# One weight group in three: the low part added up by a DMA instead of subtracted on VectorE

## The chip, the cores and the metric

The kernel runs on one core of a Trainium2 chip. The time is device microseconds of one execution, taken as the median of several runs; lower is better. TensorE (PE) multiplies, VectorE (DVE) and ScalarE (ACT) work elementwise, GpSimd (POOL) does a few small operations, and SyncE (SP) issues the loads. Sixteen DMA engines carry the transfers of all queues.

## The reference: one decoder layer on 256 tokens

The layer has a width of 2048. One projection of `x` makes the inputs of two token mixers, an mLSTM with 4 heads and a retention with 8 heads; their outputs are projected, gated, merged, projected again and normalised with the residual. A feed-forward part of width 8192 with a squared ReLU and a second norm follow:

```
u  = x @ w_in + b_in                      # 2048 -> 16392 columns
ya = head_norm(mlstm(...)) * sigmoid(mo) @ w_branch_m
yb = head_norm(retention(...)) * silu(rg) @ w_branch_r
y  = (sigmoid(ga) * ya + sigmoid(gb) * yb) @ w_out + b_out
h  = layer_norm(alpha * x + y)
out = layer_norm(alpha * h + relu(h @ w1 + b1)**2 @ w2 + b2)
```

All of it is float32. The weights of these products are some 319 MB, each read once.

## The kernel before

The float32 products are made of three passes of a shorter float format (`F32R`): each operand is split in a high part, which is the value rounded to that format, and a low part, value minus high part, and a product is high by high, low by high and high by low.

**The stream of weights.** The weights lie in memory as 608 groups of 128 x 1024 float32 (512 KB), in the order of use. `load_until` has SP load group `g` into one of four buffers `raw` (L94 to L96). `split_until` makes the two parts: ACT casts `raw` to `whi` (L111), and then DVE subtracts, `wlo = raw - whi` (L112). `whi` and `wlo` have three buffers each (`ring`, L65), so a group's parts can be made when TensorE has done with the parts of the group three places before. `next_w` (L131) asks for the split of group `g + 2` when group `g` is handed to TensorE, so parts are at most two groups ahead. A few groups at the two norms go to wider places instead of the ring (`hold`, tile name `held`).

**Two ways of use.** In `w_stationary` (L137) the weights are the stationary operand: a group is 8 pairs of matmuls, one of 512 columns with `whi` (L145) and one of 256 with `wlo` (L147), and two groups make a block of 128 output rows, followed by elementwise work on ACT and DVE (in the feed-forward part `up`: `t` L728 and L729, `sg` L732, `y` L734, `hT` L735 and L736). In `x_stationary` (L153) and `x_split` (L172) the activations are stationary and a group is 12 matmuls of 512 columns, each set of three being L164 (`whi`), L165 (`whi`), L166 (`wlo`).

**What sets the order.** Each engine works through its own list in order, and a scheduler sets where the lists' rows stand from the order of the program. Work of the heads and transposes is slipped in between groups by generators (`step`). POOL's list before holds only four constants, 16 small `pow` operations (`rstd_of`, L363) and four multiply-adds at the very end (L762, L763). SP's list holds the loads, each waiting until its buffer is free.

Of the kernel before, what the change touches and what calls it, by code (L numbers as in the profile page):

```python
# [10 lines left out]
F32 = mybir.dt.float32  # L11
F32R = mybir.dt.float32r
I32 = mybir.dt.int32
AF = mybir.ActivationFunctionType
OP = mybir.AluOpType
PSUM = bass.MemoryType.PSUM

P = 128
T = 256
D = 2048  # L20
KB = D // P
# [18 lines left out]
def layer_kernel(ctx: ExitStack, tc: tile.TileContext, xT, x, pos, wp, wg, cols, rows, b_in, b_ff1, gbias,  # L40
                 cst, decay, sel, out):
    nc = tc.nc
    V, S, TE, G = nc.vector, nc.scalar, nc.tensor, nc.gpsimd
# [10 lines left out]
    def big(name):  # L54
        return s16.tile([P, 4096], F32, tag="s16", name=name)

    def pair(name):
        return t32.tile([P, KB, 2, T], F32R, tag="t32", name=name)

# [1 line left out]
    NG = wp.shape[0]  # L61
    RAW_B, HL_B = 4, 3
    raws, parts, place = {}, {}, {}
# [1 line left out]
    def ring():  # L65
        return (wpool.tile([P, GW], F32R, tag="whi", bufs=HL_B, name="whi"),
                wpool.tile([P, GW], F32R, tag="wlo", bufs=HL_B, name="wlo"))

    def hold(first, sizes):
        for pool, n in sizes:  # L70
            box = []

            def view(i, pool=pool, n=n, box=box):
                if not box:
                    tag = {t32: "t32", s16: "s16"}[pool]
                    box.append(pool.tile([P, n, 2, GW], F32R, tag=tag, name="held"))
                return box[0][:, i, 0], box[0][:, i, 1]

            for i in range(n):
                place[first + i] = lambda i=i, view=view: view(i)  # L80
            first += n
    state = {"dma": 0, "split": 0, "use": 0}

    def pieces(g):
        n = GW // 2 if g < 3 or G_FF <= g < G_FF + 4 else GW
        return [slice(i, i + n) for i in range(0, GW, n)]

    def load_until(n):
        while state["dma"] < min(n, NG):
            g = state["dma"]  # L90
            if g < KB // 2:
                k = slice(2 * g, 2 * g + 2)
                nc.sync.dma_start(xraw[:, k], xT[:, k])
            r = wpool.tile([P, GW], F32, tag="raw", bufs=RAW_B, name="raw")  # L94
            for c in pieces(g):
                nc.sync.dma_start(r[:, c], wp[g, :, c])  # L96
            raws[g] = r
            state["dma"] += 1

    def split_until(n):  # L100
        while state["split"] < min(n, NG):
            g = state["split"]
            load_until(g + 1)
            hi, lo = place.pop(g)() if g in place else ring()
            r = raws.pop(g)
            if g < KB // 2:
                k = slice(2 * g, 2 * g + 2)
                S.copy(xs[:, k, 0], xraw[:, k])
                V.tensor_tensor(xs[:, k, 1], xraw[:, k], xs[:, k, 0].bitcast(F32), OP.subtract)
            for c in pieces(g):  # L110
                S.copy(hi[:, c], r[:, c])  # L111
                V.tensor_tensor(lo[:, c], r[:, c], hi[:, c].bitcast(F32), OP.subtract)  # L112
            parts[g] = (hi, lo)
            state["split"] += 1
            load_until(g + 1 + RAW_B)
# [15 lines left out]
    def next_w():  # L131
        g = state["use"]
        split_until(g + HL_B)
        state["use"] += 1
        return parts.pop(g)
# [62 lines left out]
        return ([(g, h) for h in range(2) for g in range(HOLD)],  # L198
                [(g, h) for g in range(HOLD, n) for h in range(2)])

# [1 line left out]
    xraw = big("xraw").rearrange("p (k t) -> p k t", k=KB)  # L202
    xs = pair("xs")
    warm = cp.tile([P, 1], F32, name="warm")
# [1 line left out]
    S.activation(warm, warm, AF.Sigmoid)  # L206
    load_until(RAW_B)
    split_until(HL_B)
    wg_t = cp.tile([P, KB, 8], F32, name="wg_t")
    nc.sync.dma_start(wg_t, wg)  # L210
# [19 lines left out]
    def rows_bc(dst, i):  # L230
        nc.sync.dma_start(dst, bass.AP(tensor=rows.tensor, offset=rows.offset + i * D, ap=[[0, P], [1, D]]))

# [1 line left out]
    ex = cp.tile([P, MH, 384], F32, name="ex")  # L234
    em = cp.tile([P, 2, MH], F32, name="em")
    cos_t = cp.tile([P, T], F32, name="cos_t")
# [119 lines left out]
        yield  # L356
        V.tensor_scalar(sin_t, sin_t, col[:, C_SIGN:C_SIGN + 1], None, OP.mult)

# [1 line left out]
    def rstd_of(dst, var, n):  # L360
        v = sm.tile([P, n], F32, tag=f"ve{n}", name="ve")
        V.tensor_scalar(v, var, EPS, None, OP.add)
        G.tensor_tensor(dst, v, nhalf[:, :n], OP.pow)  # L363
# [118 lines left out]
                V.scalar_tensor_tensor(dst[:, eb + i, 1], t, g, dst[:, eb + i, 0].bitcast(F32),  # L482
                                       OP.mult, OP.subtract)

# [1 line left out]
    def halves(t):  # L486
        return t.rearrange("p (a b) -> p a b", a=2)

# [56 lines left out]

    x_stationary(xs, KB, 4, mo_chunk)

# [1 line left out]
    hmT = []  # L549
    rqk = big("rqk").rearrange("p (k t) -> p k t", k=16)  # L550

# [25 lines left out]

    x_stationary(xs, KB, 4, rg_chunk)

# [1 line left out]
    def gate(dst, c0):  # L581
        def consume(blk, ps):
            t = wk.tile([P, T], F32, tag="t1", name="t1")
            S.activation(t, ps[:, T:], AF.Copy)
            V.tensor_tensor(t, ps[:, :T], t, OP.add)
            S.activation(dst[:, blk], t, AF.Sigmoid, bias=col[:, c0 + blk:c0 + blk + 1])
        return consume
# [4 lines left out]
    sgb = big("sgb").rearrange("p (k t) -> p k t", k=16)  # L592
    w_stationary(xs, 16, gate(sgb, C_BIN + 48))

# [1 line left out]
    hrT = []  # L596

    def branch_m(blk, ps):
# [27 lines left out]

    w_stationary(hrT[0], 16, branch_r)

# [1 line left out]
    hold(G_OUT + 24 + 8 - HOLD, [(s16, 2), (s16, 2), (s16, 2)])  # L630
    hold(G_FF, [(s16, 2), (s16, 2), (s16, 2)])
    st1 = sm.tile([P, 2, 4, 6], F32, tag="st1", name="st1", bufs=2)
# [48 lines left out]

    x_split(mgT, *late(KB), first_norm)

# [1 line left out]
    hT = pair("hT")  # L685
    brow = wk.tile([P, 512], F32, tag="brow", name="brow")
    nc.sync.dma_start(brow, bass.AP(tensor=b_ff1.tensor, offset=b_ff1.offset, ap=[[0, P], [1, 512]]))
# [18 lines left out]
    b2 = big("b2")[:, 0:D]  # L706
# [62 lines left out]
    x_split(hT, *late(KB), second_norm)  # L769


# [1 line left out]
def _stat(w):  # L773
    k, n = w.shape
    return w.reshape(k // P // 8, 8, P, n // P, P).transpose(3, 0, 2, 1, 4).reshape(-1, P, GW)


def _move(w):
    k, n = w.shape
    return w.reshape(k // P // 2, 2, P, n // 512, 512).transpose(3, 0, 2, 1, 4).reshape(-1, P, GW)  # L780


def _constants():
    s = np.arange(P)
    cst = np.zeros((P, 3, P), np.float32)
    cst[:, 0] = np.eye(P)
    cst[:, 1] = s[:, None] <= s[None, :]
    cst[:, 2] = 1.0
    lg = np.log1p(-(2.0 ** (-5.0 - np.arange(RH))))
    rel = np.arange(T)[None, :] - s[:, None]  # L790
    dec = np.where(rel >= 0, np.exp(np.maximum(rel, 0)[None] * lg[:, None, None]), 0.0) * RDQK ** -0.5
    dec = np.concatenate([dec, dec[:, :, :P]], axis=2).transpose(1, 0, 2).astype(np.float32)
    sel = np.zeros((MH, MH, P), np.float32)
    for h in range(MH):
        sel[h, h] = 1.0
    half = RDQK // 2
    invf = np.power(10000.0, -np.arange(half) / half).astype(np.float32)
    fc = np.stack([np.concatenate([invf, invf]),
                   np.concatenate([-np.ones(half), np.ones(half)]).astype(np.float32)], axis=1)
    return cst, np.ascontiguousarray(dec), sel, fc.astype(np.float32)  # L800


def _lay_out(i):
    w_in, b_in = np.asarray(i["w_in"])[0], np.asarray(i["b_in"])[0]
    w1, w2 = np.asarray(i["w_ff1"])[0], np.asarray(i["w_ff2"])[0]
    c = lambda o, n: w_in[:, o:o + n]  # noqa: E731
    parts = [_move(c(O_MV, D)), _stat(c(O_MQ, D)), _move(c(O_MO, D)), _stat(c(O_RQ, D)), _move(c(O_RV, D)),
             _move(c(O_RG, D)), _stat(c(O_GA, 2 * D)), _stat(np.asarray(i["w_branch_m"])[0]),
             _stat(np.asarray(i["w_branch_r"])[0]), _move(np.asarray(i["w_out"])[0])]
    for q in range(4):  # L810
        f = slice(q * D, (q + 1) * D)
        up = [_move(w1[:, :512]), _stat(w1[:, 512:D])] if q == 0 else [_stat(w1[:, f])]
        parts += up + [_move(w2[f])]
    wp = np.concatenate(parts, axis=0)
    x = np.asarray(i["x"])[0]
    cst, dec, sel, fc = _constants()
    b2 = lambda v: np.asarray(v).reshape(-1, P).T  # noqa: E731
    cols = np.concatenate([
        b2(b_in[O_MQ:O_MQ + D]), b2(b_in[O_RQ:O_RQ + D]), b2(b_in[O_GA:O_GA + 2 * D]),
        *[b2(np.asarray(i["m_conv_w"])[0][k]) for k in range(CONV_K)], b2(np.asarray(i["m_conv_b"])[0]),  # L820
        b2(np.asarray(i["m_norm_g"])[0]), b2(np.asarray(i["r_norm_g"])[0]), b2(np.asarray(i["b_ff1"])[0]), fc,
        b2(np.asarray(i["ln1_g"])[0]), b2(np.asarray(i["ln1_b"])[0])], axis=1)
    rows = np.stack([np.asarray(i[n])[0] for n in ("b_out", "ln1_g", "ln1_b", "b_ff2", "ln2_g", "ln2_b")])
    return {
        "xT": x.T.reshape(KB, P, T).transpose(1, 0, 2), "x": x, "pos": np.asarray(i["positions"])[0], "wp": wp,
        "wg": w_in[:, O_GI:O_GI + 8].reshape(KB, P, 8).transpose(1, 0, 2), "cols": cols, "rows": rows, "b_in": b_in, "b_ff1": np.asarray(i["b_ff1"])[0][:512],
        "gbias": b_in[O_GI:O_GI + 8], "cst": cst, "decay": dec, "sel": sel,
    }
# [15 lines left out]
```

## Time and profile before

| | before |
|---|---|
| median of 2 runs | 1762.16 us (1761.91 to 1762.40) |
| span of the profiled execution | 1760.6 us; nothing of that execution is known outside its span |
| PE busy | 1740.9 us (99%) |
| PEld busy (weight loads, beside PE) | 1475.3 us (84%) |
| DVE busy | 1111.0 us (63%) |
| ACT busy | 840.7 us (48%) |
| POOL busy | 19.7 us (1%) |
| DMA, share of 16 engines | 56.7% on the one queue of the loads |
| mean granted TensorE clock | 0.998 of 2.4 GHz |

Busy shares are means over the whole span. A row of a timeline gives the start, the duration and what the instruction makes of what. Matmul durations overlap, so the step from one start to the next is a matmul's cost.

### The profile page before, as it was taken

The numbers are of one execution on the slowest core, as the hardware profiler recorded it, in microseconds if no ns is written. First come the engines' busy times: TensorE is split into PE (matmuls) and PEld (weight loads), VectorE is DVE, ScalarE is ACT, GpSimd is POOL, SyncE is SP. The second block draws the span as 40 slices with busy tenths as digits, with TensorE's granted clock in tenths as the row PEclk, the third lists the DMA queues.
The fourth block names the chain that finished last, engine by engine and source line by source line (L and its number), as shares of the span: only waits on it lengthen the run. The fifth ranks groups of instructions, "written<-read, shape, count | busy, mean of one in ns | idle before, by whom it ended". The sixth has DMA issues, their size and how long they took to land.

```text
span 1760.6 us, 23131 instructions
## 1 busy us (share of the span) xinstructions
PE 1740.9 (99%) x8882; PEld 1475.3 (84%) x8882; DVE 1111.0 (63%) x1535; ACT 840.7 (48%) x1144; POOL 19.7 (1%) x24
## 2 busy tenths in 40 slices
PE   8999999999999999999999999999999999999997
PEld 6888888888888888888888878888888888888885
DVE  5788766875566645466666578655665566556656
ACT  5454444654444544554444465534553455345532
POOL 0000000000000000000000000000000000000001
PEclk9999999999999999999999999999999999999999
DMA  8565545456665456555555557555555555555553
GB/s 288 177 205 188 194 166 167 168 191 203 205 206 187 163 183 238 184 193 189 188 186 189 199 186 280 192 192 192 184 188 194 191 189 187 195 191 183 189 193 130
DMA packets 96439, 339.44 MB, mean 193 GB/s; under 512 B 10820, under 2 KB 12868, under 8 KB 95304
## 3 DMA queue, kind: packets, MB, share of 16 engines
q1 hardware_dynamic: 96328, 337.97, 56.7%
q8 instruction: 69, 1.13, 0.2%
q14 instruction: 42, 0.34, 0.1%
HBM read 335.83 MB, written 2.10 MB: 192 GB/s over the span
## 4 chain that ended last, share of the span: by engine, by line
PE 58%; issue 40%; DVE 1%; POOL 0%; ACT 0%; DMA 0%; SPq 0%; POOLq 0%; ACTq 0%
PE ps_w L145 20%; PE ps_w L147 10%; PE ps_x L164 8%; PE ps_x L165 8%; PE ps_x L166 8%; PE tp L475 0%; PE n L375 0%; PE ps_x L187 0%; PE ps_x L186 0%; PE ps_x L185 0%; PE n L376 0%; PE n L377 0%; PE gp L247 0%; PE sp L382 0%; DVE xr L766 0%
## 5 line engine op out<-in xcount | busy, mean ns | idle before, releaser
L112 DVE TENSOR_TENSOR wlo<-raw,whi 128x1024 fp32r<-128x1024 f32 (+1 forms) x593 | 722.7, 1219 | 545.3 <-ACT whi L111 541.8
L111 ACT CAST whi<-raw 128x1024 fp32r<-128x1024 f32 (+1 forms) x593 | 619.8, 1045 | 706.1 <-PE ps_x L165 377.2
L145 PE MATMUL ps_w<-xs,whi 128*128 128x512 f32 x1024 | 363.4, 399 | 0.0
L145 PE MATMUL ps_w<-x1T,whi 128*128 128x512 f32 x960 | 338.1, 397 | 0.0
L147 PE MATMUL ps_w<-xs,wlo 128*128 128x256 f32 x1024 | 287.6, 281 | 0.0
L147 PE MATMUL ps_w<-x1T,wlo 128*128 128x256 f32 x960 | 269.5, 281 | 0.0
L145 PEld LDWEIGHTS ps_w<-xs,whi 128*128 128x128 f32 x1024 | 192.4, 188 | 47.0
L145 PEld LDWEIGHTS ps_w<-x1T,whi 128*128 128x128 f32 x960 | 180.2, 188 | 43.9
L164 PE MATMUL ps_x<-whi,xs 128*128 128x512 f32 x512 | 201.8, 394 | 4.9 <-ACT whi L111 4.9
L165 PE MATMUL ps_x<-whi,xs 128*128 128x512 f32 x512 | 200.6, 392 | 0.0
L166 PE MATMUL ps_x<-wlo,xs 128*128 128x512 f32 x512 | 200.1, 391 | 0.0
L147 PEld LDWEIGHTS ps_w<-xs,wlo 128*128 128x128 f32 x1024 | 193.5, 189 | 0.1
L165 PE MATMUL ps_x<-whi,hT 128*128 128x512 f32 x480 | 186.8, 389 | 0.0
L164 PE MATMUL ps_x<-whi,hT 128*128 128x512 f32 x480 | 186.8, 389 | 0.0
L166 PE MATMUL ps_x<-wlo,hT 128*128 128x512 f32 x480 | 186.7, 389 | 0.0
L145 PE MATMUL ps_w<-yT,whi 128*128 128x512 f32 x512 | 181.8, 400 | 0.0
L147 PEld LDWEIGHTS ps_w<-x1T,wlo 128*128 128x128 f32 x960 | 181.4, 189 | 0.2
L147 PE MATMUL ps_w<-yT,wlo 128*128 128x256 f32 x512 | 143.8, 281 | 0.0
L164 PEld LDWEIGHTS ps_x<-whi,xs 128*128 128x128 f32 x512 | 96.8, 189 | 25.5 <-ACT whi L111 5.0
L145 PEld LDWEIGHTS ps_w<-yT,whi 128*128 128x128 f32 x512 | 96.2, 188 | 23.5
L166 PEld LDWEIGHTS ps_x<-wlo,xs 128*128 128x128 f32 x512 | 96.8, 189 | 20.6 <-DVE wlo L112 0.2
L165 PEld LDWEIGHTS ps_x<-whi,xs 128*128 128x128 f32 x512 | 96.9, 189 | 19.7
(246 smaller groups left out, 1546.5 us busy)
## 6 DMA issues: line engine op xcount, KB each, us to landing
raw<-in_wp SPq DMA_DIRECT2D x601, 512.0 KB, 3.4
brow<-in_b_in SPq DMA_DIRECT2D x16, 256.0 KB, 4.4
gb<-in_rows SPq DMA_DIRECT2D x4, 1024.0 KB, 8.2
raw<-in_wp SPq DMA_DIRECT2D x14, 256.0 KB, 4.6
xraw<-in_xT SPq DMA_DIRECT2D x8, 256.0 KB, 6.5
xr<-in_x SPq DMA_DIRECT2D x1, 2048.0 KB
dec<-in_decay SPq DMA_DIRECT2D x8, 192.0 KB, 3.1
bob<-in_rows SPq DMA_DIRECT2D x1, 1024.0 KB, 5.4
```

The source lines that it names most:

```text
L111: S.copy(hi[:, c], r[:, c])
L112: V.tensor_tensor(lo[:, c], r[:, c], hi[:, c].bitcast(F32), OP.subtract)
L145: TE.matmul(ps, hi[:, c], src[:, kb].rearrange("p a t -> p (a t)"), start=kb == 0, stop=False)
L147: TE.matmul(ps[:, :T], lo[:, c], src[:, kb, 0], start=False, stop=kb == KB - 1)
L164: TE.matmul(ps[half], src[:, kb, 0, t], hi[:, w], start=first, stop=False)
L165: TE.matmul(ps[half], src[:, kb, 1, t], hi[:, w], start=False, stop=False)
L166: TE.matmul(ps[half], src[:, kb, 0, t], lo[:, w], start=False, stop=last)
```

## The change

For each group with `g % 3 == 2`, from group 16 to group 591 and where the group is one piece, `split_until` now has ACT write the negated raw weights, rounded to the short format, into the low part's buffer, ACT cast the high part as before, and POOL issue a DMA that adds the raw weights onto the negated high part in SBUF. The subtraction on DVE is gone for these groups. This holds for 191 groups: 103 of `w_stationary`, 85 of `x_stationary` and `x_split` in the ring, and 3 held ones. Comment lines fall away elsewhere, so a line from L118 on has a number higher by 5.

```diff
-            for c in pieces(g):
-                S.copy(hi[:, c], r[:, c])
-                V.tensor_tensor(lo[:, c], r[:, c], hi[:, c].bitcast(F32), OP.subtract)
+            if g % 3 == 2 and KB <= g < NG - 16 and len(pieces(g)) == 1:
+                S.activation(lo, r, AF.Copy, scale=-1.0)
+                S.copy(hi, r)
+                G.dma_start(lo.bitcast(F32), r, accum_op=OP.add)
+            else:
+                for c in pieces(g):
+                    S.copy(hi[:, c], r[:, c])
+                    V.tensor_tensor(lo[:, c], r[:, c], hi[:, c].bitcast(F32), OP.subtract)
             parts[g] = (hi, lo)
             state["split"] += 1
             load_until(g + 1 + RAW_B)
```

The list of ACT in an `x_stationary` product of the feed-forward part, before (numbers after a name tell buffers apart):

```order
L111 CAST whi_10471<-raw_10399 128x1024
L111 CAST whi_10489<-raw_10417 128x1024
L111 CAST whi_10507<-raw_10435 128x1024
L111 CAST whi_10525<-raw_10453 128x1024
L111 CAST whi_10543<-raw_10475 128x1024
L111 CAST whi_10561<-raw_10493 128x1024
```

The same stretch of ACT's list now:

```order
L116 CAST whi_10451<-raw_10378 128x1024
L116 CAST whi_10469<-raw_10396 128x1024
L112 CAST whi_10487<-raw_10414 128x1024
L111 ACTIVATE wlo_10488<-raw_10414 128x1024
L116 CAST whi_10506<-raw_10433 128x1024
L116 CAST whi_10524<-raw_10455 128x1024
L112 CAST whi_10542<-raw_10473 128x1024
L111 ACTIVATE wlo_10543<-raw_10473 128x1024
```

One group in three has the negation (L111) right behind its cast (L112), and the groups that follow have moved down by one row.

The list of ACT in `w_stationary` of the feed-forward part (`t1` is the tile that the profile names `t`), before:

```order
L111 CAST whi_9574<-raw_9470 128x1024
L728 ACTIVATE t1_9564<-ps_w_9519 128x256
L732 ACTIVATE sg_9567<-t1_9564,col_136 128x256
L111 CAST whi_9596<-raw_9492 128x1024
L735 CAST hT_9181<-y_9569 128x256
```

The same part of the program now:

```order
L112 CAST whi_9984<-raw_9869 128x1024
L733 ACTIVATE t1_9969<-ps_w_9924 128x256
L111 ACTIVATE wlo_9985<-raw_9869 128x1024
L737 ACTIVATE sg_9972<-t1_9969,col_136 128x256
L116 CAST whi_10007<-raw_9892 128x1024
L740 CAST hT_9293<-y_9974 128x256
L116 CAST whi_10039<-raw_9929 128x1024
L733 ACTIVATE t1_10029<-ps_w_9983 128x256
L737 ACTIVATE sg_10032<-t1_10029,col_136 128x256
L111 ACTIVATE wlo_10062<-raw_9951 128x1024
L740 CAST hT_9293<-y_10034 128x256
L112 CAST whi_10061<-raw_9951 128x1024
```

Where the changed group is the first of its block, the negation stands behind `t`; where it is the second, it stands behind `sg` and ahead of `hT`, and its own cast comes two rows later. On POOL's list there is one DMA for each changed group, 191 in all, each with a wait for ACT.

## Rows read from the trace of the kernel before

**Rows 1.** The page, parts 1 and 2 (40 slices of the span).
```profile
span 1760.6 us, 23131 instructions
PE 1740.9 (99%) x8882; PEld 1475.3 (84%) x8882; DVE 1111.0 (63%) x1535; ACT 840.7 (48%) x1144; POOL 19.7 (1%) x24
...
PE   8999999999999999999999999999999999999997
...
PEclk9999999999999999999999999999999999999999
```

**Rows 2.** The page, part 4, shares of the chain that ended last.
```profile
PE 58%; issue 40%; DVE 1%; POOL 0%; ACT 0%; DMA 0%; SPq 0%; POOLq 0%; ACTq 0%
```

**Rows 3.** The page, part 5: busy us, mean ns of one, idle before.
```profile
L112 DVE TENSOR_TENSOR wlo<-raw,whi 128x1024 fp32r<-128x1024 f32 (+1 forms) x593 | 722.7, 1219 | 545.3 <-ACT whi L111 541.8
L111 ACT CAST whi<-raw 128x1024 fp32r<-128x1024 f32 (+1 forms) x593 | 619.8, 1045 | 706.1 <-PE ps_x L165 377.2
```

**Rows 4.** Timeline of an x_stationary product: start us, us, engine, line.
```profile
1317.14 0.39 PE L164 MATMUL ps_x<-whi,hT 128*128 128x512 f32 x1
...
1317.15 1.05 ACT L111 CAST whi<-raw 128x1024 fp32r<-128x1024 f32 x1 [1.67 <-PE ps_x L165]
...
1317.59 0.39 PE L166 MATMUL ps_x<-wlo,hT 128*128 128x512 f32 x1
...
1318.24 1.22 DVE L112 TENSOR_TENSOR wlo<-raw,whi 128x1024 fp32r<-128x1024 f32 x1 [1.50 <-ACT whi L111]
...
1319.86 0.39 PE L164 MATMUL ps_x<-whi,hT 128*128 128x512 f32 x1
```

**Rows 5.** Timeline of w_stationary, the `up` product of the feed-forward part.
```profile
1272.31 0.40 PE L145 MATMUL ps_w<-x1T,whi 128*128 128x512 f32 x1
...
1272.44 1.05 ACT L111 CAST whi<-raw 128x1024 fp32r<-128x1024 f32 x1 [1.23 <-issue]
...
1272.55 0.28 PE L147 MATMUL ps_w<-x1T,wlo 128*128 128x256 f32 x1
...
1273.40 0.38 ACT L728 ACTIVATE t<-ps_w 128x256 f32<-128x256 f32 x1
...
1275.12 0.51 ACT L732 ACTIVATE sg<-t,col 128x256 f32<-128x256 f32 x1 [1.35 <-DVE t L729]
...
1275.14 0.40 PE L145 MATMUL ps_w<-x1T,whi 128*128 128x512 f32 x1
```

**Rows 6.** Queues (packets, MB, share) and issues (us to landing) of DMA.
```profile
q1 hardware_dynamic: 96328, 337.97, 56.7%
...
raw<-in_wp SPq DMA_DIRECT2D x601, 512.0 KB, 3.4
...
bob<-in_rows SPq DMA_DIRECT2D x1, 1024.0 KB, 5.4
```

**Rows 7.** Tile `raw`, all its loads.
```profile
DMA to landing us min/median/max: 3.0/3.4/9.2
```

**Rows 8.** Tile `gb`, its four loads of 1024 KB.
```profile
DMA to landing us min/median/max: 4.5/8.2/10.9
```

**Rows 9.** Timeline of POOL, the shortest `pow`.
```profile
584.15 0.69 POOL L363 TENSOR_TENSOR rs<-ve,nhalf 128x2 f32<-128x2 f32 x1 [2.82 <-DVE ve L362]
```

**Rows 10.** Waits of SP's queue: us in total, times, longest.
```profile
SPq L96 <- DVE wlo L112: 857.1, 361, 7.6
```

**Rows 11.** Windows: us, busy (count) of PE, PEld, DVE, ACT, POOL, then clock, DMA.
```profile
1038.00:1040.00 2.00, 0.61 (x3) 0.19 (x2) 2.00 (x8) 2.00 (x4) 0.11 (x1) 1.00 0.00 0
...
1748.00:1750.00 2.00, 0.47 (x3) 0.05 (x1) 1.93 (x4) 0.00 (x0) 0.00 (x0) 1.00 0.70 265
1750.00:1752.00 2.00, 0.00 (x0) 0.00 (x0) 1.50 (x6) 0.00 (x0) 1.05 (x1) 0.96 0.29 112
1752.00:1754.00 2.00, 0.00 (x0) 0.00 (x0) 2.00 (x4) 0.79 (x1) 1.03 (x1) 0.50 0.00 0
```

## The prediction, made before the result was known

> **What bounds the kernel now.** I read the page's busy shares first. TensorE is busy for 1740.9 us of 1760.6, evenly over the slices, with the clock fully granted [rows 1]; all the idle time of TensorE is 20 us. The chain that ended last gives PE 58% and "issue" 40% [rows 2]; the second is the step between pipelined matmuls of the same engine, so TensorE is bound by its own matmuls. VectorE, at 63%, spends 722.7 us on the subtractions and sits idle ahead of them for 545 us until the cast on ScalarE is done; ScalarE sits idle ahead of its casts for 706 us, mostly until TensorE lets go of a buffer [rows 3]. So the split of the weights is paced by TensorE, and an engine relieved of a subtraction saves nothing. What the change can do is to make a low part late.
>
> **How much time a low part has.** Two timelines show the beat. In an x_stationary product a group begins at 1317.14 and the next at 1319.86, so a group takes 2.72 us; its first use of a low part comes 0.45 us after its start (1317.59). The cast at 1317.15 serves the group that begins two groups later, at 1322.58, and the first low matmul of that group is due at 1323.03 [rows 4]. The subtraction that starts at 1318.24 ends at 1319.46: 3.6 us to spare. In w_stationary a group takes 1275.14 - 1272.31 = 2.83 us, and the first low matmul comes 0.24 us after the start [rows 5].
>
> **The change, part by part.**
> - *Removed:* 191 subtractions of 1.22 us, 233 us of VectorE [rows 3]. Worth nothing: they end 3.6 us ahead of their use.
> - *Added on ScalarE:* 191 negations of a 128 x 1024 tile. No such row exists; the cast of the same tile takes 1.05 us [rows 4], and I take that. The 200 us bring ScalarE from 48% to 59% of the old span. Its idle time covers that, but the negation lies in the path of the low part, ahead of the DMA. A negation waits for TensorE's last use of the old low part; the casts behind it wait for a later release anyway.
> - *Added on POOL:* 191 DMAs, each waiting for the negation. The 16 `pow` operations share this queue, and some now stand behind a DMA that waits; between heads there is room for some us, at the two norms one DMA can add a negation's wait. I cost this at under 10 us.
> - *Raw buffers:* a `raw` of a changed group is freed by the landing of the accumulate and not by VectorE, and SP, which issues in order and waits now for VectorE (857 us over 361 loads, [rows 10]), waits there with the next loads behind it. Working with the landing time taken below: the accumulate that starts at 1319.25 lands 6.1 us later, at 1325.35; the load that reuses the buffer takes 3.4 [rows 6] and lands at 1328.75. Its cast is four groups after 1317.15, at 1328.03, plus the stall of 2.3 us that this landing causes, 1330.3. So it stays hidden, by 1.6 us.
>
> **The path of a changed low part.** From the negation's end to the first low matmul, the DMA has:
> - x_stationary: cast 1317.15 to 1318.20, negation to 1319.25, due at 1323.03: **3.78 us**.
> - w_stationary, first group of a block (52 groups): cast from 1272.44, then `t`, which ends at 1273.78, negation to 1274.83; due at 1272.31 + 5.66 + 0.24 = 1278.21: **3.38 us**.
> - w_stationary, second group (51): the negation stands behind `sg`, which ends at 1275.63, and ends at 1276.68; its old buffer is free from 1275.14; due at 1275.14 + 5.66 + 0.24 = 1281.04: **4.36 us**.
> - The 3 held groups don't wait for a ring buffer: no stall.
>
> If the time L from the negation's end to the landing is longer than that, TensorE waits for the rest, once in each changed group: the negation of the next changed group waits until TensorE has gone through this one, so a stall is never made up.
>
> **What L is.** No row shows an accumulating DMA or one issued by POOL. Below, L is no less than the fastest plain load of the same 512 KB, 3.0 us [rows 7]. Above, I take the slowest 1024 KB load among other loads, 10.9 us [rows 8], and a POOL operation of 0.69 us for the issue [rows 9], 11.6 in all. The nearest row is the 1024 KB load that landed in 5.4 us [rows 6], since an accumulate of 512 KB reads the raw tile and the old low part, 1024 KB. With 0.7 us for the issue on POOL, **L = 6.1 us**.
>
> The Trainium skill, page "DMA: Bandwidth & Descriptors", section "Anatomy of one DMA — SWDGE (gpsimd) path", fits a DMA issued by GpSimd as 2.0 us plus its bytes at 436 GB/s. By that my estimate for 512 KB is 3.2 us, the accumulate would be hidden in all three places and the time would be 1762 us; for 1024 KB it is 4.4 us. No run here shows such a DMA yet.
>
> **The sum.** With L = 6.1 a stall is 2.32 us in x_stationary (85 groups), 2.72 us and 1.74 us in w_stationary (52 and 51):
>
> 85 x 2.32 + 52 x 2.72 + 51 x 1.74 = 197 + 141 + 89 = 427 us.
>
> Span 1760.6 + 427 = 2188 us. The runs' median lies 1.6 us over the profiled span, so 2190 us. The `pow` waits of under 10 us are within the range.
>
> **Rivals.**
> 1. *Not slower: the accumulate lands in time.* The point of decision is L of 3.4 to 4.4 us. For it: plain loads land in 3.0 to 3.4 us, and the DMA engines are free 43% of the time [rows 6, 7]. Against it: these numbers are for half the bytes read, and from a queue that needs no work of POOL. At L of 3.4 or less no group stalls, and the time is 1762 us; VectorE's freed 233 us give nothing. At L = 4.0 the sum is 52 x 0.62 + 85 x 0.22 = 51 us, which is 1813 us. That rule of the Trainium skill (the page on DMA, same section) is this rival's mechanism. Chance 0.11, of which 0.01 lies between 2% slower and 1813 us.
> 2. *Much slower: the adding itself is slow.* 96328 packets took 56.7% of 16 engines, 166 ns each [rows 6]; a tile of 128 rows is 8 packets on each engine, 1.3 us. At twice that for an accumulate, it adds 191 x 2.66 = 507 us to 998 us of each engine, which is still under the span. If adding needs four or more times a packet, or if POOL is slow to make up the DMA, L goes to 8 and more; at the bound of 11.6 the stalls are 7.82, 8.22 and 7.24 us, 1461 us in all, so 3223 us. At such gaps TensorE's clock can fall as well: after the last matmul, in 1748 to 1750, the grant was 0.96 in the next two us and then 0.50, which is 1.2 GHz, while 1.4 us of idle time in 1038 to 1040 left it at 1.00 [rows 11]. At the lower level a group takes another 2.72 us; once in each changed group that would be 520 us more, part of which the next DMA gets back as time to land. Gaps of 2.3 us lie between those rows, and I count the clock as kept there. Chance 0.09.
> 3. *In between, by the lock of a port.* VectorE is busy 63%, with 1.22 us operations [rows 1, 3]; if POOL had to wait for the end of one each time it makes up a DMA, L is up to 7.3 and the sum up to 188 x 1.2 = 226 us more, 2415 us. I have no row for such a wait. It is part of the forecast's range. The Trainium skill, page "SBUF — State Buffer", section "🔬 SBUF: two separate sides", says that GpSimd can't write descriptors during VectorE's two-port modes; no run here shows it.
>
> That the change does nothing it says can be left out: POOL's list has the 191 DMAs, and VectorE's has 191 subtractions fewer.
>
> **How the numbers follow.** The forecast, that the accumulate lands late and TensorE waits in each of the 188 ring groups, has a chance of 0.80, with L between 4.0 and 9.6 us. These ends give 1813 us (above) and 85 x 5.82 + 52 x 6.22 + 51 x 5.24 = 1085 us, 2848 us. With the 0.11 below and 0.09 above left out, the range is 1810 to 2850 us. A change of 2%, 35 us, is about what a measurement of this kernel tells from none. That is L of about 3.9, so slower has 0.80 + 0.09 + 0.01, less 0.01 that I keep for something that I don't see on the faster side: 0.89; same 0.10; faster 0.01.
>
> **What the profile after would show.** Right: a queue of POOL's DMAs with 191 issues of 512 KB landing in about 6 us; waits of the low matmuls (L171, L152) for that DMA, some 188 of 1.7 to 2.7 us each, and hardly any others; PE's busy share near 1741 of 2188, 80%; clock at 1.00; the negations at 1.05 us; subtractions on VectorE down by 191. Wrong: landing under 3.4 us and PE at 99% (rival 1); landing of 8 us and more or a clock below 1.00 in the steady stretches (rival 2); negations of much more than 1.05 us, casts that wait for a late `raw` load, or waits for the `pow` operations as the larger part of PE's idle time, each of which would put the loss in a step that I cost at nothing.

## The result and the profile after

The changed kernel takes **2047.05 us** (median of two runs, 2043.15 to 2050.95) against 1762.16 us: a ratio of **1.161, 95% interval 1.1595 to 1.1633**. The prediction was 2190 us, with a range of 1810 to 2850. The profiled execution has a span of 2041.4 us, 280.8 us more than before.

Parts 1 and 2 of the page of the changed kernel (it answers to [rows 1]):

```profile
span 2041.4 us, 23487 instructions
...
PE 1798.6 (88%) x8882; PEld 1478.5 (72%) x8882; DVE 892.9 (44%) x1344; ACT 1024.0 (50%) x1335; POOL 185.4 (9%) x215
...
PE   8988899988899888888888877988888998889987
```

TensorE still does the same 8882 matmuls, but slices of 8 have taken the place of the even row of 9s: its idle time went from 19.7 us (1760.6 - 1740.9) to 242.8 (2041.4 - 1798.6). That is 223.1 of the 280.8 us; its busy time grew by the other 57.7. VectorE fell to 44%, and no time was gained by it.

What TensorE waits for (engine, line, releaser: us in total, times, longest), changed kernel:

```profile
PE ps_w L152 <- DMA wlo<-raw: 122.2, 82, 6.7
PE ps_x L171 <- DMA wlo<-raw: 81.6, 73, 2.2
PE ps_x L192 <- DMA held<-raw: 10.9, 3, 6.3
...
PE ps_x L192 <- DMA wlo<-raw: 3.9, 2, 2.7
```

These are the low matmuls of the three kinds of product (L152 in `w_stationary`, L171 and L192 in x-stationary products), and what they wait for is the accumulating DMA. The four rows hold 218.6 of the 242.8 us.

The queues and the issues (packets, MB, share of 16 engines; then xcount, KB, median us from issue to landing), which answer to [rows 6]:

```profile
q1 hardware_dynamic: 96328, 337.97, 46.4%
q0 software_dynamic: 27504, 100.15, 27.0%
...
raw<-in_wp SPq DMA_DIRECT2D x601, 512.0 KB, 4.2
wlo<-raw POOLq DMA_DIRECT2D x188, 512.0 KB, 4.7
...
held<-raw POOLq DMA_DIRECT2D x3, 512.0 KB, 9.1
```

The accumulates land 4.7 us after the start of their issue, and the raw loads take 4.2 us instead of 3.4.

The costliest groups of the split (busy us, mean ns of one, idle before; they answer to [rows 3]):

```profile
L117 DVE TENSOR_TENSOR wlo<-raw,whi 128x1024 fp32r<-128x1024 f32 (+1 forms) x405 | 492.8, 1217 | 685.8 <-ACT whi L116 682.5
...
L113 POOL DMA_DIRECT2D wlo<-raw x188 | 162.7, 865 | 1700.5 <-ACT wlo L111 1375.6
...
L111 ACT ACTIVATE wlo<-raw 128x1024 fp32r<-128x1024 f32 x188 | 198.2, 1054 | 55.3 <-PE ps_w L152 53.2
```

The negation takes 1.05 us, as taken. POOL is busy 0.86 us for one issue, where 0.7 had been taken.

One changed group from cast to use, in an `x_stationary` product (timeline: start us, us, engine, line):

```profile
1532.15 1.05 ACT L112 CAST whi<-raw 128x1024 fp32r<-128x1024 f32 x1
...
1533.10 1.05 ACT L111 ACTIVATE wlo<-raw 128x1024 fp32r<-128x1024 f32 x1
...
1534.45 0.86 POOL L113 DMA_DIRECT2D wlo<-raw  x1 [8.45 <-ACT wlo L111]
...
1537.80 0.39 PE L170 MATMUL ps_x<-whi,hT 128*128 128x512 f32 x1
...
1539.21 0.50 PE L171 MATMUL ps_x<-wlo,hT 128*128 128x512 f32 x1 [1.02 <-DMA wlo<-raw]
...
1539.54 0.39 PE L169 MATMUL ps_x<-whi,hT 128*128 128x512 f32 x1
```

The negation ends at 1534.15, POOL starts 0.30 us later, and the low matmul starts at 1539.21, as soon as the accumulate has landed: L, the time from the negation's end to the landing, is 5.06 us here. Against the budget of 3.78 us this makes 1.28 us. The bracket shows only 1.02, since the idle time is counted from the modelled end of the matmul before. The other 0.26 us is in the busy time: that last matmul drains for 0.39 us where a step is 0.23 (0.16 more), and the first after the stall takes a step of 0.33, from 1539.21 to 1539.54 (0.10 more). So the delay of a stall is its idle time and 0.26 us.

**The account of the 280.8 us.** By place, idle time for the accumulate was 85.5 us in 85 groups of x-stationary products (median 1.02, 10 without a wait), 89.2 in 52 first groups of a block of `w_stationary` (median 1.55, 3 without) and 33.0 in 51 second groups (median 0.50, 18 without): 207.7 us. The held groups make 10.9. Draining and refilling at 160 stalls of 0.26 us each makes 42 us of busy time. A lower clock makes 17 us more: I summed busy time times what lacked of the full grant, over all stretches of 1 us with a grant under 0.90. These terms are 278 us; idle time of other kinds grew by 4.5 more (242.8 - 218.6 = 24.2, from 19.7). That is the 281 to within 1 or 2 us.

**Where the clock fell.** The longest stall, with the issue of its accumulate and a load of 2 MB ahead of it (timeline), and then windows (us, busy and count of PE, PEld, DVE, ACT, POOL, clock, DMA share, GB/s):

```profile
764.96 0.42 SPq L614 DMA_DIRECT2D xr<-in_x  x1
...
769.46 0.86 POOL L113 DMA_DIRECT2D wlo<-raw  x1 [9.02 <-ACT wlo L111]
...
779.43 0.58 PE L152 MATMUL ps_w<-xs,wlo 128*128 128x256 f32 x1 [6.74 <-DMA wlo<-raw]
```

```profile
774.00:776.00 2.00, 0.00 (x0) 0.00 (x0) 1.07 (x2) 0.51 (x1) 0.00 (x0) 0.70 0.93 254
776.00:778.00 2.00, 0.00 (x0) 0.00 (x0) 0.00 (x0) 0.00 (x0) 0.00 (x0) 0.50 1.08 274
...
782.00:784.00 2.00, 2.00 (x7) 1.69 (x7) 0.00 (x0) 0.00 (x0) 0.00 (x0) 0.50 0.65 256
```

The accumulate takes 10 us beside the large load (DMA share about 1), TensorE stands for 6.74 us, and the clock falls to 0.50 (1.2 GHz) and stays there for over 5 us after work has begun again: 7 matmuls in 2 us, where 13 stand at 1.00 (1040 to 1042). Five other stalls, of 2.75 to 6.71 us, stand behind a slow accumulate of the same kind, and behind four of them the clock falls too. But a short one can do it as well. Its matmul, and the windows behind it:

```profile
1046.56 0.39 PE L152 MATMUL ps_w<-yT,wlo 128*128 128x256 f32 x1 [2.06 <-DMA wlo<-raw]
```

```profile
1046.00:1048.00 2.00, 1.44 (x8) 1.31 (x9) 1.72 (x4) 0.00 (x0) 0.00 (x0) 0.97 0.78 274
1048.00:1050.00 2.00, 2.00 (x7) 1.72 (x7) 0.00 (x0) 0.00 (x0) 0.00 (x0) 0.50 0.94 363
```

Here the clock was 1.00 through the stall and fell after it, for about 3 us. Two stretches of this kind are in the trace (from 1048 and 1068 us), beside some 150 short stalls after which it stayed at 1.00. A third short stretch, from 71 us, has no stall just ahead of it: the last one (1.27 us) had ended at 61.01, and what ran just before the fall were small matmuls on 4 partitions (L314 and L319, from 69.17 to 71.22), and in the kernel before the same matmuls left the clock at 1.00. Eight stretches, five and three, hold the 17 us.

### The profile page after: what moved, and what is told of

It is laid out like the page before. It is cut to its first block, busy times and chain, and to the rows that moved or that the text cites. A ratio compares the mean times of both kernels' runs of the same rounds, so it can differ in the third digit from the quotient of the medians.

```text
span 2041.4 us, 23487 instructions
## 1 busy us (share of the span) xinstructions
PE 1798.6 (88%) x8882; PEld 1478.5 (72%) x8882; DVE 892.9 (44%) x1344; ACT 1024.0 (50%) x1335; POOL 185.4 (9%) x215
## 3 DMA queue, kind: packets, MB, share of 16 engines
q0 software_dynamic: 27504, 100.15, 27.0%
q8 instruction: 69, 1.13, 0.2%
## 5 line engine op out<-in xcount | busy, mean ns | idle before, releaser
L117 DVE TENSOR_TENSOR wlo<-raw,whi 128x1024 fp32r<-128x1024 f32 (+1 forms) x405 | 492.8, 1217 | 685.8 <-ACT whi L116 682.5
L116 ACT CAST whi<-raw 128x1024 fp32r<-128x1024 f32 (+1 forms) x405 | 422.1, 1042 | 349.7 <-PE ps_x L170 175.9
L112 ACT CAST whi<-raw 128x1024 fp32r<-128x1024 f32 x188 | 197.3, 1050 | 425.8 <-PE ps_x L170 215.4
L152 PE MATMUL ps_w<-xs,wlo 128*128 128x256 f32 x1024 | 292.1, 286 | 49.6 <-DMA wlo<-raw 49.1
L113 POOL DMA_DIRECT2D wlo<-raw x188 | 162.7, 865 | 1700.5 <-ACT wlo L111 1375.6
L152 PE MATMUL ps_w<-x1T,wlo 128*128 128x256 f32 x960 | 274.3, 286 | 44.5 <-DMA wlo<-raw 43.6
L152 PEld LDWEIGHTS ps_w<-xs,wlo 128*128 128x128 f32 x1024 | 194.7, 190 | 62.4 <-DMA wlo<-raw 62.2
L171 PE MATMUL ps_x<-wlo,xs 128*128 128x512 f32 x512 | 203.9, 399 | 33.7 <-DMA wlo<-raw 33.5
L111 ACT ACTIVATE wlo<-raw 128x1024 fp32r<-128x1024 f32 x188 | 198.2, 1054 | 55.3 <-PE ps_w L152 53.2
L171 PE MATMUL ps_x<-wlo,hT 128*128 128x512 f32 x480 | 191.1, 398 | 39.3 <-DMA wlo<-raw 39.3
L152 PEld LDWEIGHTS ps_w<-x1T,wlo 128*128 128x128 f32 x960 | 182.1, 190 | 57.5 <-DMA wlo<-raw 57.3
L152 PE MATMUL ps_w<-yT,wlo 128*128 128x256 f32 x512 | 147.1, 289 | 29.6 <-DMA wlo<-raw 29.6
L171 PEld LDWEIGHTS ps_x<-wlo,xs 128*128 128x128 f32 x512 | 96.7, 189 | 66.7 <-DMA wlo<-raw 46.8
```

The source lines that it names most:

```text
L111: S.activation(lo, r, AF.Copy, scale=-1.0)
L112: S.copy(hi, r)
L113: G.dma_start(lo.bitcast(F32), r, accum_op=OP.add)
L152: TE.matmul(ps[:, :T], lo[:, c], src[:, kb, 0], start=False, stop=kb == KB - 1)
L171: TE.matmul(ps[half], src[:, kb, 0, t], lo[:, w], start=False, stop=last)
```

## Experiments

The expectations number the theories. **Theory 1** is the prediction's: a changed low part is late because cast, negation, POOL's start and the landing lie one behind the other, and the landing time is a given. **Theory 2** says that the landing time is not a given: loads that run at the same time stretch it. **Theory 4**, which came up after the first experiment, is that the later release of the raw buffers holds back the loads (the chain of buffers). **Theory 3**, that ScalarE's longer list makes the casts late, is tried in `neg_only`. All kernels were timed beside the kernel before, which ran in 1762.0 to 1762.5 us.

**early: start the accumulate one group earlier.** The negation and the DMA of a changed group go out right behind the split of the group ahead of it; for that the ring of low parts has one buffer more, and three small tiles (`brow`, `pr`, `zp`) have one buffer instead of two.

```diff
+    def start_low(g):
+        load_until(g + 1)
+        ahead[g] = lo_tile()
+        S.activation(ahead[g], raws[g], AF.Copy, scale=-1.0)
+        G.dma_start(ahead[g].bitcast(F32), raws[g], accum_op=OP.add)
...
+            if g + 1 < NG and g + 1 not in place and by_dma(g + 1):
+                start_low(g + 1)
```

> The changed kernel, with the negation and the accumulate of a changed group started one group earlier: the low part has a fourth buffer (paid for by single buffers of the tiles brow, pr and zp), the high part is cast where it was. The 3 held groups stay as they were. Theory 1 (a path that is too long: the accumulate lands some 5.0 us after the negation, against 3.4 to 4.4 us until it is due): due 2.7 to 2.8 us later, it lands in time in nearly all groups; what is left are the held groups and the accumulates that run beside a load of 1 or 2 MB, some 40 us with the lower clock behind them. 1800 us (1775 to 1830). Theory 2 (the DMA engines: the accumulates and the loads get in each other's way, and an earlier start only makes them wait there): landing goes to 6 us and more, 1950 us or more.

Measured: 2105.11 us, ratio 1.196 (1.1902 to 1.2012): slower than the changed kernel, though the low part had the time of one group (2.7 us) more. The landing itself went from 4.7 us to 9.0, and the largest wait of TensorE grew. One issue, that wait, and a piece of the timeline:

```profile
wlo<-raw POOLq DMA_DIRECT2D x188, 512.0 KB, 9.0
```

```profile
PE ps_w L177 <- DMA wlo<-raw: 140.6, 86, 4.1
```

```profile
1531.80 0.86 POOL L83 DMA_DIRECT2D wlo<-raw  x1 [7.92 <-ACT wlo L82]
...
1541.85 0.39 PE L177 MATMUL ps_w<-x1T,wlo 128*128 128x256 f32 x1 [2.10 <-DMA wlo<-raw]
```

This accumulate is issued at 1531.80 and lands 10 us later. What the queues did in the first 5 us of it, and in the second 5 (packets, MB, share of 16 engines; q1 holds SP's loads, q0 the accumulates):

```profile
q1 hardware_dynamic: 315, 1.16, 79.5%
q0 software_dynamic: 3, 0.01, 1.2%
```

```profile
q0 software_dynamic: 141, 0.51, 52.0%
q1 hardware_dynamic: 117, 0.41, 26.7%
```

It does not run slowly: of its 144 packets 3 run in the first half and 141 in the second, once the loads' packets have thinned out. Over 14 changed groups from 1400 us on, the mean share of q0 was 0, 4 and 10% in the second, third and fourth us after the issue, with q1 at 98, 88 and 74%; q0's turn came in the sixth to eighth us (61, 81, 66%). In the changed kernel, over the same stretch, q0 had 68, 101 and 114% in the second to fourth us (a share adds up the times of packets, and can pass 100), and q1 1, 0 and 0%. There the loads are gone when the accumulate starts, since SP stands at raw buffers that are not yet free. The two largest waits of SP's queue in the changed kernel (they answer to [rows 10]):

```profile
SPq L96 <- DVE wlo L117: 644.7, 216, 9.5
SPq L96 <- DMA wlo<-raw: 619.4, 187, 13.3
```

So theory 1 missed by its fixed landing time, and theory 2 has to be put more sharply: the accumulate waits for its turn while loads are under way. These need not have come before it. At 950.70 an accumulate was issued with no load under way, and SP issued three right behind it; in the second and third us q1 had this, and q0 no packet:

```profile
950.70 0.86 POOL L83 DMA_DIRECT2D wlo<-raw  x1 [7.86 <-DVE wlo L140]
950.76 1.29 SPq L112 DMA_DIRECT2D raw<-in_wp  x3
```

```profile
q1 hardware_dynamic: 105, 0.43, 97.9%
```

From the fourth us on both queues ran (q0 at 51 and 65%, q1 at 59 and 33%). Theory 4 has a part too. The negations now wait for loads that come late:

```profile
ACT wlo L82 <- DMA raw<-in_wp: 62.6, 64, 5.9
```

If each of these negations came earlier by its wait, at most 39 us of TensorE's waits would go (the smaller of the wait and the stall, summed over the groups; an estimate). A late load can't stretch the landing, which is counted from the issue on. TensorE's waits for accumulates came to 249 us instead of 219. The mean clock was 0.970, with 34 stretches at the lower level, 58 us by the sum used above instead of 17.

**dve_neg: the negation on VectorE.** It takes 694 ns there and does not stand behind the cast.

```diff
-                S.activation(lo, r, AF.Copy, scale=-1.0)
+                V.tensor_scalar(lo, r, -1.0, None, OP.mult)
```

> The changed kernel with the negation on VectorE, so that it runs beside ScalarE's cast and not behind it. Theory 1: the negation ends about 1.0 us earlier in the x_stationary product and up to 1.5 us earlier in w_stationary, so the stalls (medians 1.0, 1.55 and 0.5 us) are nearly gone, apart from those beside large loads: 1820 us (1790 to 1860). Theory 2 (DMA engines): no change, 2040 us.

Measured: 1986.03 us, ratio 1.125 (1.1214 to 1.1293). It gains 61 us on the changed kernel, about a quarter of what was expected. The medians of the stalls are 0.57, 0.70 and 0.59 us at the three places. Its issues:

```profile
raw<-in_wp SPq DMA_DIRECT2D x601, 512.0 KB, 4.4
wlo<-raw POOLq DMA_DIRECT2D x188, 512.0 KB, 5.4
```

0.7 us of what the path became shorter went to a longer landing, as theory 2 has it (over 14 groups from 1400 us on, q1 was still at 64% in the second us after the issue and q0 at 29%, then q0 at 101 and 104%), and lower clock cost 29 us (14 stretches) against 17. The stalls of the second groups did not shrink at all (33.9 us in sum, from 33.0); why was not followed up.

**plain_pool: the same DMA without the adding.**

```diff
-                G.dma_start(lo.bitcast(F32), r, accum_op=OP.add)
+                G.dma_start(lo.bitcast(F32), r)
```

> The changed kernel with a plain copy of the raw tile by POOL's DMA in place of the accumulate; the adding is left out, so the low parts hold the raw weights. If reading two tiles sets the landing time of 4.7 us, a plain copy lands 1 us or more earlier, near the 3.4 us of a load, and the time goes to 1850 us or less. If the queue of POOL and its fixed costs set it, it lands within 0.3 us of 4.7 and the time stays over 1980 us.

Measured: 1814.06 us, ratio 1.029 (1.0268 to 1.032, two executions). Of its page, and of POOL in its timeline:

```profile
q0 software_dynamic: 27504, 100.15, 13.7%
...
wlo<-raw POOLq DMA_DIRECT2D x188, 512.0 KB, 2.9
```

```profile
1380.81 0.53 POOL L113 DMA_DIRECT2D wlo<-raw  x1 [7.91 <-ACT wlo L111]
```

The adding alone is worth 1.8 us of the landing and 233 us of the time (2047 - 1814), so it is not the queue of POOL that sets the landing. Whether the second read or the addition itself takes the time, this run doesn't tell. The same packets take 0.144 us each (13.7% of 16 engines over 1809.2 us, by 27504), and 0.320 us when they add (27.0% of 2041.4): 2.2 times. POOL's issue is 0.53 us instead of 0.86. TensorE's idle time for this DMA is 4.2, 18.5 and 3.4 us at the three places: nearly hidden.

**neg_only: the negation stays, the subtraction comes back** (VectorE makes the low part over the negated tile; no DMA).

```diff
-                G.dma_start(lo.bitcast(F32), r, accum_op=OP.add)
+                V.tensor_tensor(lo, r, hi.bitcast(F32), OP.subtract)
```

> The changed kernel with VectorE's subtraction in place of the accumulate: ScalarE's negation is still made and then written over. Theory 1: ScalarE's extra 200 us cost nothing by themselves, since the low part is ready 2.5 us ahead of its use: 1762 to 1775 us. Theory 3 (ScalarE's longer list makes the casts late): 1850 us or more.

Measured: 1762.60 us, ratio 1.0002 (0.9993 to 1.0012). ScalarE is busy 1024.1 us, 58%, as much as in the changed kernel, and it costs nothing: theory 3 falls. The loss hangs on the DMA.

**halves: negation and accumulate in two halves of 512 columns.**

```diff
-                S.activation(lo, r, AF.Copy, scale=-1.0)
+                for c in (slice(0, GW // 2), slice(GW // 2, GW)):
+                    S.activation(lo[:, c], r[:, c], AF.Copy, scale=-1.0)
+                    G.dma_start(lo[:, c].bitcast(F32), r[:, c], accum_op=OP.add)
```

> The changed kernel with the negation and the accumulate of a changed group in two halves of 512 columns, each an ACTIVATE and a DMA of 256 KB of its own. Theory 1 (a path that is too long by 0.7 to 1.6 us): the first half starts 0.45 us earlier and moves half as much, and the second is due half a group, 1.36 us, later; the stalls of the ring groups are nearly gone, those beside large loads stay: 1830 us (1790 to 1880). Theory 2 (what sets the landing are the loads beside it): the loads now meet two transfers, and the gain is half of that or less: 1930 us or more.

Measured: 1915.90 us, ratio 1.088 (1.0862 to 1.0899): between the two forecasts. Half the bytes land in nearly the same time:

```profile
wlo<-raw POOLq DMA_DIRECT2D x376, 256.0 KB, 4.5
```

The first half starts 0.4 us earlier (the half negation takes 0.62 us), but the two together move the same bytes, and POOL issues one half behind the other (1.75 us for both), so the second half starts 0.4 us later than a whole one would. The smallest landing of a half is 3.3 us and the median 4.5. This does not decide between the theories: of the 1.2 us between them a part may be the other half and a part loads.

**apart: six groups left to VectorE,** those of the six longest stalls.

```diff
-            if g % 3 == 2 and KB <= g < NG - 16 and len(pieces(g)) == 1:
+            if g % 3 == 2 and KB <= g < NG - 16 and g not in (230, 266, 350, 356, 359, 362) and len(pieces(g)) == 1:
```

> The changed kernel without the accumulate in 6 of the 191 groups (230, 266, 350, 356, 359 and 362), whose accumulates ran beside a load of 1 or 2 MB or into a held place and made TensorE wait 2.8 to 6.7 us each, 31.7 us in all, with the granted clock at 0.50 after the longest. They are split by VectorE as before. If each of those stalls costs its idle time and some 2 us of lost clock, the time is 2047 - 32 - 10 = 2005 us (1990 to 2020). If a stall is only handed on to the next changed group, less than 15 us are saved.

Measured: 2013.76 us, ratio 1.143 (1.1383 to 1.1469), as expected. 33 us for six groups, 5.5 us each, where a changed group costs 1.5 us on average (280.8 by 191). The slowest landing of a ring group went from 11.3 to 6.3 us. The clock stays at 1.00 in the six places, but nine other short stretches at the lower level cost 16 us in the profiled execution, as much as in the changed kernel: what the six groups give back is idle time (242.8 to 215.4 us), not clock.

**sixth and sixth_second: half of the changed groups.** Of the changed groups of `w_stationary`, the one has only first groups of a block, the other only second ones; they have 96 and 95 groups in all.

```diff
-            if g % 3 == 2 and KB <= g < NG - 16 and len(pieces(g)) == 1:
+            if g % 6 == 2 and KB <= g < NG - 16 and len(pieces(g)) == 1:
```

> The changed kernel with every sixth group changed and not every third, 95 groups. If each changed group pays by itself, half of the 285 us are left: 1905 us (1880 to 1930). If the cost comes from the load of the DMA engines and of the queues as a whole, it falls by much more than half: under 1850 us.

```diff
-            if g % 3 == 2 and KB <= g < NG - 16 and len(pieces(g)) == 1:
+            if g % 6 == 5 and KB <= g < NG - 16 and len(pieces(g)) == 1:
```

> The changed kernel with every sixth group changed, those with g % 6 == 5, 95 groups; in w_stationary all of them are the second group of their block, where those with g % 6 == 2 (1930 us) are all the first. Theory 1 (a stall is the path less the time until the part is due): the second groups have 1 us more, so they cost some 0.8 us each and not 1.8, and 51 x 0.8 + 43 x 1.3 = 97 us: 1860 us (1835 to 1880). If the place in the block does not matter and every changed group pays alike: 1930 us.

Measured: 1930.04 us (ratio 1.095, 1.093 to 1.0973, two executions), at the upper edge, and 1889.94 us (1.0724, 1.0708 to 1.074), above what was expected. Their waits, `sixth` first:

```profile
PE ps_w L152 <- DMA wlo<-raw: 87.3, 49, 6.6
PE ps_x L171 <- DMA wlo<-raw: 38.2, 34, 2.2
```

```profile
PE ps_w L152 <- DMA wlo<-raw: 51.6, 48, 5.7
PE ps_x L171 <- DMA wlo<-raw: 42.9, 40, 2.2
```

Both have the landing of the changed kernel, 4.7 us. First groups cost more than second ones, as their budgets say (3.38 and 4.36 us), and the two losses, 168 and 128 us, make 296 where the changed kernel loses 285: nearly all of a stall is paid by its own group. First groups wait 87.3 us here and 89.2 in the changed kernel, and those of x-stationary products 83.7 (39.3 and 44.4) and 85.5. But the 51 second groups wait 51.6 us here and 33.0 there, so first groups' stalls do give something back to them. In the changed kernel their negation stands ready when TensorE lets go of the old buffer (ScalarE is idle 53.2 us for that, in the row of L111 above); here it stands right behind `sg` (3.4 us idle ahead of all 94), and in `up` the low part is due 4.3 us after the negation at the median, against 4.9 there. So the size was off for second groups (median 1.01 us, not 0.5, which was the median of the changed kernel). It differs by stage as well: in `up` their stalls are 0.55 us at the median and in the other stages 1.13, where other work stands in ScalarE's list (budget 3.7 and 3.6 us at the median in the stages of `conv_silu` and `branch_r`).

**early_thin: early, with fewer loads.** One raw load in three is gone in most of the program, and its group uses one fixed tile; but the raw ring is one buffer shorter, and a changed group still holds its buffer until the landing. Theory 2 wants the accumulate fast again, theory 4 does not.

```diff
+            if thin(g):
+                raws[g] = fixed
+                state["dma"] += 1
+                continue
+            if sum(1 for k in raws if not thin(k)) >= RAW_B - 1:
+                return
```

> The kernel with the accumulate one group earlier, which was slower (2105 us, landing 9.0 us), with the raw tile of nearly every group with g % 3 == 1 left unloaded: those groups split one fixed raw tile, so a third of the weight traffic and the right weights of those groups are left out. The order of buffers and waits stays: a load still waits for the accumulate that reads its buffer. Theory 2 (loads beside the accumulate stretch its landing from 4.7 to 9.0): landing falls to 6 or 7 us and the time under 1900 us. Theory 4 (the chain load, negation, accumulate, next load through the few raw buffers is too long by itself): landing stays near 9 and the time stays over 2000 us.

Measured: 1796.62 us, ratio 1.019 (1.0174 to 1.0215, two executions). Issues, a wait of TensorE, and SP's wait:

```profile
raw<-in_wp SPq DMA_DIRECT2D x414, 512.0 KB, 4.0
wlo<-raw POOLq DMA_DIRECT2D x188, 512.0 KB, 4.6
```

```profile
PE ps_w L189 <- DMA wlo<-raw: 7.0, 4, 4.7
```

```profile
SPq L124 <- DMA wlo<-raw: 1308.6, 187, 15.6
```

With 414 loads instead of 601 the accumulate lands in 4.6 us again (q0 at 63, 102 and 104% in the second to fourth us, over 14 groups from 1260 us on), and TensorE waits 7 us for it in these matmuls where `early` waited 140.6 (17.8 and 248.5 in all). Theory 2 stands. SP still waits 1308.6 us for the accumulates, but no negation of the ring waits for a load any more: with fewer loads the chain of buffers is looser too, so this run alone doesn't tell what theory 4 had of the loss in `early`.

**early_sixth: early, for every sixth group.** The edit is that of `early` with `g % 6 == 5` in `by_dma`.

> The same 95 groups with the negation and the accumulate one group earlier. Theory 2 with theory 1: with half of the accumulates the loads are less crowded, the landing stays under the 6.5 to 7.1 us that an accumulate then has, and the stalls are gone but for some beside large loads: 1770 us (1760 to 1790), within 2% of the kernel before. If an early start always runs into the loads and lands after 9 us, as in the kernel with 191 of them: 1950 us or more.

Measured: 1866.14 us, ratio 1.059 (1.0567 to 1.061), neither of the two. Landing is 7.3 us, though only one negation waited for a load (2.8 us), so it is not theory 4:

```profile
wlo<-raw POOLq DMA_DIRECT2D x94, 512.0 KB, 7.3
```

This is 24 us better than `sixth_second`, but one early accumulate in six groups still meets loads: over 14 groups from 1400 us on q0 had 5 and 24% in the second and third us, and 88 and 96% in the next two. Theory 2 has the direction; how much later the turn comes it had not said. No version beat the kernel before, and none pointed to one: TensorE is busy 99% there. More raw buffers were not tried.

## Why the prediction was right, and which term was off

The mechanism was right: the accumulate lands late, TensorE waits, and a stall is hardly made up (18.6 us of second groups' waits apart, see `sixth_second`). The term that was mis-sized is **L**.

- *L.* Taken 6.1 us (5.4 to land and 0.7 on POOL), measured 5.0 at the median (5.01, 5.06 and 4.84 at the three places): 0.30 until POOL starts, and 4.7 from there, the 0.86 us on POOL included. The nearest row, a load of 1024 KB, was a fair neighbour and 0.7 us too long; the issue was to be counted in the landing and not ahead of it. The Trainium skill, page "DMA: Bandwidth & Descriptors", section "Anatomy of one DMA — SWDGE (gpsimd) path", gave estimates of 3.2 us for 512 KB and 4.4 for 1024 KB: the first is close to `plain_pool` (2.9), the second to the accumulate (4.7, against 4.5 for the fastest). So counting the bytes of both operands was the better guess here; that it is the reading, and not the addition, that takes the time is not shown.
- *The budgets* held at the median: 3.77, 3.27 and 4.42 us, against 3.78, 3.38 and 4.36. With L = 5.0 they give 85 x 1.22 + 52 x 1.62 + 51 x 0.64 = 104 + 84 + 33 = 221 us, instead of 427. Measured with the 0.26 us of each stall are 85.5 + 20 = 105, 89.2 + 13 = 102 and 33.0 + 9 = 42. The first is right; in the second are three of the long stalls. The budget of the third was read in one stage; it is 4.9 us at the median in that stage and 3.5 to 3.8 in three others (`conv_silu`, `branch_m`, `branch_r`).
- *Terms that lacked,* by the account: the 18 us of long stalls and the 9 of the third budget, just told, 11 us at the three held groups, which I had at no stall, since the accumulates of held groups landed only after 9.1 us; 17 us of clock. They gave back some of the 206 us by which L was too dear, so the forecast of the time was better than that of L, and that part is luck.
- *The subtraction* is worth nothing: VectorE went to 44%. *The negation's* 200 us of ScalarE are worth nothing by themselves (`neg_only`); in the path they count, as `dve_neg` shows.
- *Raw buffers* stayed hidden: TensorE's one long wait for a cast is 5.6 us at the start (4.9 without the change). The `pow` operations cost nothing: none is among what TensorE waits for.
- *The signs.* 188 stalls of 1.7 to 2.7 us were to be seen; 157 were there in ring groups, of 1.3 us on average. PE's busy share was to be 80% and is 88%. Clock at 1.00 was wrong in eight stretches that cost 17 us.
- *Rival 1* (lands in time) fell by 0.6 to 1.6 us, and was near for second groups, where 18 of 51 didn't wait. `plain_pool` shows how it would have looked.
- *Rival 2* (adding is slow, the clock falls) was right on the packet, 0.320 us against 0.144, about the twice that I took and not four times (9 packets on each engine, not 8), and the price on the path that it was to bring, a landing of 8 us and more with the clock down behind it, came in a few places only. `early`, at 9.0 us, shows it as the rule, by loads and not by the adding.
- *Rival 3* (the lock of a port) did not happen: POOL's issue takes 852 to 1017 ns with VectorE busy or not, median 862, and starts 0.30 us after the negation. The rule on descriptors of the Trainium skill's page "SBUF — State Buffer", section "🔬 SBUF: two separate sides", is one for VectorE's two-port modes. No run here shows that these subtractions use one, so the rule was not put to the test.

## What to carry to other kernels

An operation that is moved off an idle-rich engine into a DMA is judged by its latency on the path, from the release of its input to the landing, against the slack of its first use in each stage. A DMA that adds is dearer than the same copy: here 0.320 us a packet against 0.144, and 1.8 us more to landing. Starting it earlier helps only if no loads are under way there: look at what the other queue is doing in the new place before counting the time gained.

## What the runs showed of the hardware

- An accumulate's 144 packets take some 3 us of all 16 engines, and hardly one ran while loads kept the engines busy (3 of 144 in the first 5 us at 1531.80, with q1 at 79.5%), even loads issued just behind it (950.70, for 3 us; then both queues ran). Landing is 4.7 us with few loads about, 7.3 and 9.0 us behind some, and 10 behind a load of 2 MB. What sets this order between the two queues is open.
- POOL's issue of a DMA takes 0.86 us with the adding, 0.53 without, and begins 0.30 us after its releaser.
- A stall costs TensorE 0.26 us beyond the idle time that the profile shows, as read at 1539.21; 160 times that and the 17 us of clock make 59 us, and its busy time grew by 57.7.
- Short stalls (1.4 us on average) left the clock at 1.00 nearly always; behind two of them, of 1.80 and 2.06 us, it went to 0.50 for about 3 us. [Rows 11] had shown neither. What tells the two apart is open.
